# Moving stores from SyncE's queue to ScalarE's, pinning loads, and a diagonal-free spread in a streaming encoder layer

## The chip, the cores and the metric

The kernel runs on one core of a Trainium2 chip. Its time is the device time of one execution in microseconds (us); it is given as the median of several runs. A profile is one execution taken by the hardware profiler. The engines are PE (TensorE; PEld is its weight load), DVE (VectorE), ACT (ScalarE), POOL (GpSimd) and SP (SyncE, which here only issues DMAs). A DMA is issued by an instruction on an engine's own queue, SPq or ACTq; that instruction waits, in its place in the queue, until what it reads or overwrites is ready.

## The reference

One layer of a streaming encoder over 2048 prompt tokens and 64 sample tokens of width 1024, then a final RMSNorm. The first half mixes tokens (pooling and a matrix memory); the change leaves it as it is. The second half, which the change touches, is this:

```python
    h2 = rmsnorm(x, g2) * (1 + sc2) + sh2
    up = h2 @ w_up                      # 1024 -> 2 * 2816
    upp = jnp.concatenate([conv_buf.astype(up.dtype), up], 1)
    conv = b_conv + sum(w_conv[j] * upp[:, j:j + T] for j in range(CONV_W))
    a, g = jnp.split(conv, 2, -1)
    x = x + gt2 * ((jax.nn.silu(g) * a) @ w_down)
    ...
    y_prompt = rmsnorm(xp, g_final)
    y_sample = rmsnorm(xs, g_final)
```

`rmsnorm(x, g)` is x times the reciprocal root of its mean square over the 1024 features, times g. All is float32.

## The kernel before

Features lie on partitions and tokens run along the free dimension. The mixing half goes through four groups of 512 tokens and leaves the residual rows x in a DRAM tensor `x2d` (8 blocks of 128 features). The feed-forward half goes through three groups (`fgroups`, `o.g` = 0, 1, 2) of 704 tokens.

**Precision and pieces.** Every matmul operand is split into a high and a low part, and a product is three passes (`PASSES`) of float32r matmuls. A weight piece of 512 columns is loaded by SP, copied by ACT into its high part (`work_out`, L359), and DVE subtracts to get the low part (L362). The split piece lies in one of six buffers of the tag `wt`.

**The stream.** `stream` lists all weight pieces in the order in which PE wants them. `issue` starts the DMA of the next one: `w_up` and `w_down` pieces go through one of four `raw` buffers (L343), sums of `w_up` blocks (`wsum`) go straight into a `wt` buffer (L351), and pieces that were split before and kept come back whole (`wsplit`, L348). `pump` runs ahead: it splits the next few pieces and issues loads while fewer than six `wt` buffers are in use and at most seven pieces are pending. `get_unit` hands the next piece to PE, and `keep` (L367) stores it to DRAM if a later group is to load it whole. In group 0 of the feed-forward half two of the four `wsum` pieces of each feature block are kept this way, 44 stores of 512 KB.

**A pair.** For each of 22 feature blocks f, `Pair.products` computes the up projection of the a and g halves for 704 tokens with seven products in place of eight (sums of blocks, as in Strassen's scheme). A product is 12 matmuls of 352 columns (L1443). They follow each other as B11, B21, T4 of the pair before, T2, T3, B22, T1 (the first pair of a part has no T4). The kept pieces are those of T2 and T1. Between the products ACT copies PSUM banks (L1482, L1491, L1506), DVE adds and applies the convolution taps (L1451, L1495, L1431), ACT does scale and silu, and the result is split into `av`. `product` calls `pump` first, then `get_unit`, and after every second of its four blocks calls `tick(0)`.

**Parts.** The 22 blocks come in four parts (5, 5, 6, 6). After each part `down` multiplies its `av` by the `w_down` pieces (L1709), and `down_end` adds the result, times gt2, to the residual rows `x3` (L1724). `x3` has eight tiles, one buffer each (tags x0 to x7). `load_x2` (L1578) loads them from `x2d`: in group 0 two after each of the first pairs; in groups 1 and 2 two after each pair of part 0 once the list `bg[0]` is empty, and the rest at the end of part 0.

**Background work.** `bg` holds lists of generators; `tick(i)` runs the first one of list i up to its next `yield`, `drain` runs it to the end. `final`, for groups 0 and 1, is put into `bg[0]` at the end of a group and thus runs during part 0 of the next: it gets the mean square of each token (L1597), spreads the factor to all partitions, and for each of eight k multiplies `x3[k]` in place (DVE, L1606), stores it to the output `yT` (SP, L1608) and yields four times. `load_x2` for the next group therefore writes the very tile that L1608 reads. `prepare`, for groups 1 and 2, makes the next group's normed input and stores pieces of it from ACT (L784).

**The end.** The last part of group 2 does its down projection in two sections of tokens (`ENDS`, 448 and 256). `final_end` makes the output of a section; that of the first is ticked during the last five rows of the second, for every second of the six k of a row, and what is left runs in the last `drain`. It sums squares per token on PE (L1623), takes the factor `rs` on DVE and POOL (L1587, L1589), writes a diagonal matrix of it (DVE, L1630), multiplies it by ones on PE (L1637), which spreads the factor over the partitions, copies it (ACT, L1639), and multiplies the rows (DVE L1660, POOL L1656). `store` (L1652) sends them off.

**Order.** In the feed-forward half the instructions of PE, ACT, DVE and POOL stand in the order of the program (`tc.manual_schedule`, L1676), and so do the DMAs that ACT issues. The order of SP's queue is chosen by the framework's scheduler, which may move a DMA ahead of others that were traced before it. `tc.keep_in_program_order(ins)` ties an instruction behind the one traced before it on its engine.

Of the kernel before, what the change touches and what calls it, by code (L numbers as in the profile page):

```python
# [9 lines left out]
F32 = mybir.dt.float32  # L10
F32R = mybir.dt.float32r
AF = mybir.ActivationFunctionType
ALU = mybir.AluOpType
# [3 lines left out]
P = 128  # L17
D = 1024
KD = D // P
# [6 lines left out]
FT = 704  # L26
# [33 lines left out]
def tile_layer(ctx: ExitStack, tc: tile.TileContext, xT, vecs, cst, rst, rowv, w_mod, w_ada, w_qkou, w_v, w_pool,  # L60
               w_out, w_up, w_down, st_C, st_pool, yT, o_pool, o_C, o_m, o_conv):
    nc = tc.nc
    act, dve, pool, pe = nc.scalar, nc.vector, nc.gpsimd, nc.tensor
# [19 lines left out]
    def m2_ps():  # L83
        return bank("m2")
# [9 lines left out]
    def scr():  # L94
        return sp.tile([P, TMAX], F32, tag="scr", name="scr")
# [33 lines left out]
    ident = cp.tile([P, P], F32, tag="ident", name="ident")  # L129
# [9 lines left out]
    ones = ones_r.bitcast(F32)  # L139
# [91 lines left out]
    for g in range(NG):  # L231
        o = Grp()
# [70 lines left out]
    for g in range(NFG):  # L303
        for (f0, f1_) in PARTS:
# [8 lines left out]
            for i, (n, k) in enumerate(order):  # L313
                if i == f1_ - f0 - 2:
                    stream += late
                c = f0 + k // 4 * 4
# [9 lines left out]
    class Unit:  # L326

        state = 0
        w = raw = None
# [25 lines left out]
    def work_out(u, upto=2):  # L355
# [5 lines left out]
        if u.state == 1 and upto > 1:  # L361
            dve.tensor_tensor(out=u.w[:, 1, :u.n], in0=u.raw[:, :u.n], in1=u.w[:, 0, :u.n].bitcast(F32), op=ALU.subtract)  # L362
            u.state = 2

    def keep(u):
        if u.keep is not None:
            nc.sync.dma_start(out=u.keep, in_=u.w.bitcast(F32)[:, :, :u.n])  # L367

    def pump():

        while True:
            for i, u in enumerate(pend[:ahead[1]]):
                if u.w is not None or live[0] < ahead[2] or u.stays:
                    work_out(u, 2 if i < ahead[1] - ahead[3] else 1)
            if (pos[0] >= len(stream) or len(pend) >= ahead[0] or live[0] >= ahead[2]
                    or sum(u.w is None for u in pend) >= RB
                    or pos[0] < n_att and sum(u.w is not None for u in pend) >= WB - 2):
                break
            issue()
# [142 lines left out]
    x2d = dr.tile([KD, P, NTOK], F32, tag="x2d", name="x2d")  # L522
# [67 lines left out]
    for g in range(NFG):  # L590
        o = Grp()
# [8 lines left out]
    def fscr(dt=F32):  # L600
        if dt in ("rb", "ssum"):
            return spare[0].tile([P, FT], F32, tag=dt, name=dt)
        return spare[0].tile([P, FT], dt, tag="fscr", name="fscr", bufs=6)


    spare = []
# [182 lines left out]
    if True:  # L789
# [110 lines left out]
        h, pb = [], []  # L900
# [424 lines left out]
        for o in groups:  # L1325
# [14 lines left out]
            if o.g == 0:  # L1340
                dve.tensor_copy(M[:, GT + 1:GT + 2], RV[:, 2:3])
                dve.tensor_scalar(out=GH, in0=V[:, V_GH:V_GH + NH], scalar1=0.5, scalar2=None, op0=ALU.mult)
                t = scr()
                nc.sync.dma_start(out=t[:36, :512], in_=cst[:36, NCST + 512:NCST + 1024])
                dve.tensor_copy(E_r.rearrange("p h n -> p (h n)"), t[:36, :512])
                t = scr()
# [227 lines left out]
    def load_x2(o, ks=range(KD)):  # L1574
        x3 = []
        for k in ks:
            x = f2.tile([P, FT], F32, tag=f"x{k}", name=f"x{k}")
            nc.sync.dma_start(out=x, in_=x2d[k, :, o.t0:o.t0 + FT])  # L1578
            x3.append(x)
        return x3  # L1580

# [9 lines left out]
    def final(o, x3, ssum):  # L1591
        for _ in range(4):
            yield
        ps = m2_ps()
        tiles = [(t, min(P, FT - t)) for t in range(0, FT, P)]
        for ti, (t, n) in enumerate(tiles):
            pe.matmul(ps[:n, ti:ti + 1], ssum[:, t:t + n], ones[:, 0:1], start=True, stop=True)  # L1597
        stat_cols(ps, RF, [n for (t, n) in tiles])
        yield
        yield  # L1600
        box = []
        yield from bcast_cols(RF, 0, FT, box, fscr)
        yield
        yield
        for k in range(KD):
            dve.scalar_tensor_tensor(out=x3[k], in0=x3[k], scalar=V[:, V_GF + k:V_GF + k + 1], in1=box[0],  # L1606
                                     op0=ALU.mult, op1=ALU.mult)
            nc.sync.dma_start(out=yT[k, :, o.t0:o.t0 + FT], in_=x3[k])  # L1608
            for _ in range(4):
                yield  # L1610

    def final_end(o, x3, sums, lo, hi):

        w = hi - lo
        tiles = [(t, min(P, hi - t)) for t in range(lo, hi, P)]
        for _ in range(4 if lo == 0 else 0):
            yield
        ps = m2_ps()
        rs = f1.tile([P, 5], F32, tag="rs", name="rs", bufs=2)
        dg = fscr()  # L1620
        for ti, (t, n) in enumerate(tiles):
            for i, (sq, base) in enumerate(sums):
                pe.matmul(ps[:n, ti:ti + 1], sq[:, t - base:t - base + n], ones[:, 0:1], start=(i == 0),  # L1623
                          stop=(i == len(sums) - 1))
        stat_cols(ps, rs, [n for (t, n) in tiles])
        nf, rem = w // P, w % P
        blks = [(0, nf, P), (nf, nf + 1, rem)] if rem else [(0, nf, P)]
        for (a, b, n) in blks:
            v = dg[:n, a * P:a * P + (b - a) * n].rearrange("p (t c) -> p t c", c=n)
            dve.tensor_tensor(out=v, in0=ident[:n, :n].unsqueeze(1).broadcast_to([n, b - a, n]),  # L1630
                              in1=rs[:n, a:b].unsqueeze(2).broadcast_to([n, b - a, n]), op=ALU.mult)
        for _ in range(4 if lo == 0 else 0):
            yield
        pb = m2_ps()
        for (a, b, n) in blks:
            c = slice(a * P, a * P + (b - a) * n)
            pe.matmul(pb[:, c], ones[:n, :], dg[:n, c], start=True, stop=True)  # L1637
        rb = fscr()
        act.activation(rb[:, :w], pb[:, :w], AF.Copy)  # L1639
        YG = ((0, 1), (1, 3), (3, 5), (5, 6), (6, 8))  # L1640
        y = {}
        for (a, b) in YG:
            if a % 2 == 0 or b - a == 2:
                t = f1.tile([P, XT], F32R, tag="hx", name="y", bufs=2 * len(BN)).bitcast(F32)[:, :3 * w].rearrange(
                    "p (k t) -> p k t", t=w)
                j = 0
            for k in range(a, b):
                y[k] = (t, j)
                j += 1

        def store(a, b):
            (nc.sync if a < 5 else nc.scalar).dma_start(  # L1652
                out=yT[a:b, :, o.t0 + lo:o.t0 + hi].rearrange("k p t -> p k t"), in_=y[a][0][:, y[a][1]:y[a][1] + b - a, :w])
        if lo > 0:
            for k in (5, 6, 7):
                pool.tensor_tensor(out=y[k][0][:, y[k][1], :w], in0=x3[k][:, lo:hi], in1=rb[:, :w], op=ALU.mult)  # L1656
        for (a, b) in YG:
            for k in range(a, b):
                if k < 5 or lo == 0:
                    dve.tensor_tensor(out=y[k][0][:, y[k][1], :w], in0=x3[k][:, lo:hi], in1=pb[:, :w], op=ALU.mult)  # L1660
                    if lo == 0:
                        yield
                        yield
            store(a, b)
        yield
# [11 lines left out]
    x3, ssum = [], None  # L1677
    for o in fgroups:
        Bo = B[o.g]
        for pi, (f0, f1_) in enumerate(PARTS):  # L1680
            nf = f1_ - f0
# [4 lines left out]
            for f in range(f0, f1_):  # L1686
                old, pair = pair, Pair(o, Bo, f, f - f0, av)
                pair.products(old)
                if o.g == 0 and len(x3) < KD or pi == 0 and not bg[0]:
                    x3 += load_x2(o, range(len(x3), min(len(x3) + 2, KD)))  # L1690
            if pi == 0 and o.g > 0:
                drain(0)
                x3 += load_x2(o, range(len(x3), KD))
# [76 lines left out]
        if not o.last:  # L1770
            drain(1)
            bg[0].append(final(o, x3, ssum))
            x3 = []
# [84 lines left out]
```

## Time and profile before

| what | value |
|---|---|
| median of 3 runs | 2237.66 us (2231.12 to 2242.47) |
| the profiled execution | 2240.48 us, span 2238.7 us |
| granted TensorE clock, mean | 0.994 |
| DMA | 493.52 MB, mean 220 GB/s |
| kept pieces stored from SP in group 0 (`wsplit<-wt`) | 44 of 512 KB |
| output rows stored from SP in groups 1 and 2 (`yT<-x`) | 16 of 352 KB |
| residual rows loaded (`x<-x2d`) | 24 of 352 KB |

The span runs from the first to the last instruction; the execution's own time is a little longer. A row of the busy times gives us, share of the span and count. A row of the waits says which line on which engine stood idle, what ended the wait, how long in all, how often, and the longest. A row of the timeline begins with start and duration; the square bracket holds the idle time before it. For DMAs the time from issue to landing is counted apart from the issuing instruction.

### The profile page before, as it was taken

How to read it: one execution, taken by the hardware profiler on the slowest of the kernel's cores; microseconds unless marked ns; L12 is line 12 of the kernel's file. 1: busy time of each engine (PE TensorE's matmuls, PEld its weight loads, DVE VectorE, ACT ScalarE, POOL GpSimd, SP SyncE). 2: the span in 40 equal slices, each digit the busy share in tenths (PEclk: the TensorE clock that was granted, in tenths of full speed). 3: DMA queues.
4: the chain of work that ended last, by engine and by line, in shares of the span. 5: the costliest groups of instructions: out<-in, count | busy, mean ns of one | idle time of the engine just before them, and what ended most of it. 6: DMA issues, size and time to landing. Idle time of an engine off the chain costs nothing.

```text
span 2238.7 us, 38008 instructions
## 1 busy us (share of the span) xinstructions
PE 2196.5 (98%) x13720; PEld 2082.8 (93%) x13720; DVE 1577.7 (70%) x2860; ACT 1002.1 (45%) x1992; POOL 284.2 (13%) x524
## 2 busy tenths in 40 slices
PE   8999999999999999999999999999999999999998
PEld 6778888878898999999999999999999999999997
DVE  4868668667755688687868677687757685757474
ACT  3544335234234356464636445445435353435254
POOL 0122012111200130010100110000001210101012
PEclk9999999999999999999999999999999999999999
DMA  9967986997888477556746964556458554353442
GB/s 351 328 231 244 342 296 230 316 305 249 272 293 273 155 241 250 191 194 240 227 157 214 300 226 165 201 187 224 142 171 267 192 201 160 114 174 123 144 151 79
DMA packets 276444, 493.52 MB, mean 220 GB/s; under 512 B 24952, under 2 KB 103416, under 8 KB 276256
## 3 DMA queue, kind: packets, MB, share of 16 engines
q1 hardware_dynamic: 266784, 468.77, 62.4%
q10 hardware_dynamic: 9472, 22.32, 2.6%
q8 instruction: 108, 1.77, 0.3%
q14 instruction: 80, 0.66, 0.1%
HBM read 382.77 MB, written 108.22 MB: 219 GB/s over the span
## 4 chain that ended last, share of the span: by engine, by line
PE 83%; DMA 8%; DVE 5%; issue 2%; ACT 1%; SPq 1%; POOL 0%; POOLq 0%; DVEq 0%; ACTq 0%
PE mm L1443 38%; PE mm L1709 22%; PE mm L415 17%; DMA raw<-w_ada 2%; PE mm L1038 1%; DMA wsum<-w 1%; DMA wt<-wsum 1%; DMA wt<-hl_kept 1%; DMA hl_kept<-wt 1%; DVE acc L196 1%; DMA w<-w_ada 1%; PE m L1222 1%; PE mm L969 1%; PE m L1221 1%; PE m L1302 1%
## 5 line engine op out<-in xcount | busy, mean ns | idle before, releaser
L1443 PE MATMUL mm<-hx,wt 128*128 128x352 f32 x5544 | 886.2, 321 | 5.8 <-ACT wt L359 3.7
L1443 PEld LDWEIGHTS mm<-hx,wt 128*128 128x128 f32 x5544 | 880.7, 188 | 7.0 <-ACT wt L359 4.3
L1709 PE MATMUL mm<-av,wt 128*128 128x352 f32 (+2 forms) x3168 | 508.1, 321 | 0.0
L1709 PEld LDWEIGHTS mm<-av,wt 128*128 128x128 f32 x3168 | 502.7, 188 | 1.8 <-DVE x L1724 0.3
L415 PE MATMUL mm<-hl,wt 128*128 128x512 f32 (+2 forms) x1920 | 399.8, 361 | 4.9 <-DMA wt<-hl_kept 3.8
L362 DVE TENSOR_TENSOR wt<-raw,wt 128x512 fp32r<-128x512 f32 (+3 forms) x494 | 309.3, 642 | 90.6 <-ACT wt L359 85.5
L415 PEld LDWEIGHTS mm<-hl,wt 128*128 128x128 f32 x1920 | 316.6, 190 | 54.7 <-issue 8.5
L359 ACT ACTIVATE wt<-raw 128x512 fp32r<-128x512 f32 (+3 forms) x494 | 271.1, 570 | 189.0 <-PE mm L1709 81.0
L1724 DVE SCALAR_TENSOR_TENSOR x<-mm,MOD,x 128x352 f32<-128x352 f32 (+4 forms) x224 | 106.4, 525 | 114.8 <-PE mm L1709 114.8
L415 PE MATMUL mm<-mx,wt 128*128 128x512 f32 (+2 forms) x960 | 185.7, 353 | 1.5 <-DVE wt L362 1.3
L415 PEld LDWEIGHTS mm<-mx,wt 128*128 128x128 f32 x960 | 158.7, 188 | 26.6 <-DVE wt L362 1.5
L1431 DVE SCALAR_TENSOR_TENSOR tg<-eg,V,tg 128x704 f32<-128x704 f32 (+1 forms) x132 | 125.6, 952 | 45.6 <-ACT tg L1426 43.2
L362 DVE TENSOR_TENSOR wt<-wt 128x512 fp32r<-128x512 f32 x176 | 122.6, 697 | 45.5 <-ACT wt L359 45.5
L359 ACT ACTIVATE wt<-wt 128x512 fp32r<-128x512 f32 x176 | 110.1, 626 | 74.0 <-DMA wt<-wsum 65.7
L1431 DVE SCALAR_TENSOR_TENSOR ta<-ea,V,ta 128x704 f32<-128x704 f32 (+1 forms) x132 | 125.6, 952 | 8.5 <-ACT ta L1426 6.2
L1566 DVE TENSOR_TENSOR av<-tg,av 128x704 fp32r<-128x704 f32 (+4 forms) x112 | 62.1, 588 | 47.7 <-ACT av L1558 47.5
L196 DVE SCALAR_TENSOR_TENSOR acc<-raw,CA,acc 128x512 f32<-128x512 f32 x84 | 62.4, 775 | 41.2 <-DMA raw<-w_ada 41.2
L1537 ACT ACTIVATE tg<-tg 128x704 f32<-128x704 f32 (+1 forms) x66 | 52.4, 794 | 79.1 <-DVE tg L1431 79.1
L1451 DVE TENSOR_TENSOR eg<-mm,u 128x352 f32<-128x352 f32 x154 | 70.1, 467 | 22.8 <-ACT u L1506 11.2
L1491 ACT ACTIVATE u<-mm 128x352 f32<-128x352 f32 x66 | 30.5, 462 | 120.2 <-PE mm L1443 82.5
L1038 PE MATMUL mm<-wt,hl 128*128 128x256 f32 (+1 forms) x576 | 71.4, 282 | 2.5 <-DVE scr L578 2.5
L1038 PEld LDWEIGHTS mm<-wt,hl 128*128 128x128 f32 x576 | 69.3, 188 | 3.6 <-DVE scr L578 2.7
(281 smaller groups left out, 2030.5 us busy)
## 6 DMA issues: line engine op xcount, KB each, us to landing
wt<-hl_kept SPq DMA_DIRECT2D x108, 512.0 KB, 6.0
raw<-w_up SPq DMA_DIRECT2D x198, 256.0 KB, 3.1
wt<-wsum SPq DMA_DIRECT2D x176, 256.0 KB, 4.1
wt<-wsplit SPq DMA_DIRECT2D x88, 512.0 KB, 4.0
raw<-w_down SPq DMA_DIRECT2D x96, 256.0 KB, 2.9
w<-w_up SPq DMA_DIRECT2D x88, 256.0 KB, 4.1
wsum<-w SPq DMA_DIRECT2D x44, 512.0 KB, 4.3
wsplit<-wt SPq DMA_DIRECT2D x44, 512.0 KB, 4.8
```

Of the source, the lines that this page charges most:

```text
L196: dve.scalar_tensor_tensor(out=acc[s], in0=w, scalar=CA[:, k, s:s + 1], in1=acc[s], op0=ALU.mult, op1=ALU.add)
L359: act.activation(u.w[:, 0, :u.n], u.raw[:, :u.n], AF.Copy)
L362: dve.tensor_tensor(out=u.w[:, 1, :u.n], in0=u.raw[:, :u.n], in1=u.w[:, 0, :u.n].bitcast(F32), op=ALU.subtract)
L415: pe.matmul(ps[bi][:, :hi - lo], U[:, a, k % 4 * P:(k % 4 + 1) * P], mv[k][:, b, lo:hi], start=(at == 0 and pi == 0), stop=(k == order[-1] ...
L1038: pe.matmul(ps[ti][:n, :cols], h[4 * kh + k4][:, b, lo:lo + n], U[:, a, k4 % 2 * cols:(k4 % 2 + 1) * cols], start=(kh == 0 and k4 == 0 and ...
L1431: dve.scalar_tensor_tensor(out=t[:, :E], in0=ext[:, j:j + E], scalar=wc(j, f), in1=t[:, :E], op0=ALU.mult, op1=ALU.add)
L1443: pe.matmul(ps[:, :FH], U[:, a, kc * P:(kc + 1) * P], Bo.at(nm, kc, b), start=(first and kc == 0 and pi == 0), stop=(kc == 3 and pi == 2), ...
L1451: dve.tensor_tensor(out=ext[:, d:d + b - a], in0=ps[:, a:b], in1=u[:, a:b], op=ALU.add)
L1537: act.activation(self.tg[:, :E], self.tg[:, :E], AF.Silu)
L1566: dve.tensor_tensor(out=cut(1), in0=self.of_tg(cut(0), a, b), in1=cut(0).bitcast(F32), op=ALU.subtract)
L1709: pe.matmul(ps[i][:, :hi - lo], U[:, a, k % 4 * P:(k % 4 + 1) * P], av[k](b, lo, hi), start=(k == 0 and (a, b) == PASSES[0]), stop=(k == n ...
L1724: dve.scalar_tensor_tensor(out=x3[n][:, a:b], in0=ps[i][:, a - lo:b - lo], scalar=gt2(n, s), in1=x3[n][:, a:b], op0=ALU.mult, op1=ALU.add)
```

## The change

There are four edits, all of the feed-forward half.

1. `keep` no longer stores at once in this half. It puts the piece on the list `owed`, and the next `pump`, that is, the beginning of the next product, issues the store from ACT (`settle`). In the mixing half (`spare` still empty) nothing changes.
2. In `load_x2` the loads of groups 1 and 2 are tied behind what SP was given before them, and three rows in place of two follow each pair.
3. In `final` the store of an output row is issued by ACT, one yield after its product; the yields stay four in all.
4. In `final_end` the diagonal matrix is left out: one matmul per 128 tokens takes the column of factors, repeated 128 times, as the stationary operand and the identity as the moving one. For the first section one of four yields ahead of the spread goes, and one of two after each row.

```diff
+    owed = []
+
     def keep(u):
-        if u.keep is not None:
+        if u.keep is None:
+            return
+        if spare:
+            owed.append(u)
+        else:
             nc.sync.dma_start(out=u.keep, in_=u.w.bitcast(F32)[:, :, :u.n])
 
+    def settle():
+        while owed:
+            u = owed.pop(0)
+            act.dma_start(out=u.keep, in_=u.w.bitcast(F32)[:, :, :u.n])
+
     def pump():
 
+        settle()
         while True:
...
             x = f2.tile([P, FT], F32, tag=f"x{k}", name=f"x{k}")
-            nc.sync.dma_start(out=x, in_=x2d[k, :, o.t0:o.t0 + FT])
+            got = nc.sync.dma_start(out=x, in_=x2d[k, :, o.t0:o.t0 + FT])
+            if o.g > 0:
+                tc.keep_in_program_order(got)
...
-            nc.sync.dma_start(out=yT[k, :, o.t0:o.t0 + FT], in_=x3[k])
-            for _ in range(4):
+            yield
+            act.dma_start(out=yT[k, :, o.t0:o.t0 + FT], in_=x3[k])
+            for _ in range(3):
                 yield
...
-        dg = fscr()
...
-        nf, rem = w // P, w % P
-        blks = [(0, nf, P), (nf, nf + 1, rem)] if rem else [(0, nf, P)]
-        for (a, b, n) in blks:
-            v = dg[:n, a * P:a * P + (b - a) * n].rearrange("p (t c) -> p t c", c=n)
-            dve.tensor_tensor(out=v, in0=ident[:n, :n].unsqueeze(1).broadcast_to([n, b - a, n]),
-                              in1=rs[:n, a:b].unsqueeze(2).broadcast_to([n, b - a, n]), op=ALU.mult)
-        for _ in range(4 if lo == 0 else 0):
+        for _ in range(3 if lo == 0 else 0):
             yield
         pb = m2_ps()
-        for (a, b, n) in blks:
-            c = slice(a * P, a * P + (b - a) * n)
-            pe.matmul(pb[:, c], ones[:n, :], dg[:n, c], start=True, stop=True)
+        for ti, (t, n) in enumerate(tiles):
+            pe.matmul(pb[:, t - lo:t - lo + n], rs[:n, ti:ti + 1].broadcast_to([n, P]), ident[:n, :n],
+                      start=True, stop=True)
...
                     if lo == 0:
                         yield
-                        yield
...
-                    x3 += load_x2(o, range(len(x3), min(len(x3) + 2, KD)))
+                    x3 += load_x2(o, range(len(x3), min(len(x3) + (3 if o.g else 2), KD)))
```

## The prediction

> **What bounds the kernel now.** First the page's busy times, then busy time by stretch (columns: stretch, length, then busy time and count of PE, PEld, DVE, ACT, POOL, then granted clock, share of the DMA engines, GB/s), then PE's own waits.
>
> ```profile
> PE 2196.5 (98%) x13720; PEld 2082.8 (93%) x13720; DVE 1577.7 (70%) x2860; ACT 1002.1 (45%) x1992; POOL 284.2 (13%) x524
> ...
> 828.70:1291.00 462.30, 461.45 (x2912) 461.00 (x2913) 351.39 (x565) 242.12 (x423) 46.16 (x97) 1.00 0.66 221
> 1291.00:1758.50 467.50, 465.19 (x2926) 464.60 (x2925) 333.48 (x538) 218.91 (x390) 38.14 (x97) 1.00 0.59 198
> 1758.50:2226.90 468.40, 466.98 (x2946) 464.70 (x2944) 313.26 (x591) 208.96 (x392) 62.38 (x191) 1.00 0.43 145
> 2217.00:2239.00 22.00, 12.43 (x89) 10.79 (x89) 9.76 (x27) 4.87 (x11) 6.87 (x10) 0.77 0.38 131
> ```
>
> The feed-forward half is the three stretches from 828.7, one per group of 704 tokens. PE is busy in all but 0.85, 2.31 and 1.42 us of them: TensorE bounds this half, and the change takes no work worth counting off TensorE. So it can win only those idle microseconds, what follows from them, and part of the tail, where PE is busy 12.43 of 22. PE's waits in narrow windows name the idle time (waiting line, what it waited for, us, times, longest):
>
> ```profile
> PE mm L1443 <- DVE ea L1495: 0.8, 1, 0.8
> PE mm L1443 <- ACT wt L359: 2.3, 1, 2.3
> PE mm L1443 <- ACT wt L359: 1.4, 1, 1.4
> ```
>
> These are the window 938 to 950 (group 0), 1285 to 1340 (group 1) and 1755 to 1830 (group 2). The second is followed by a slow stretch:
>
> ```profile
> 1331.30:1334.70 3.40, 3.40 (x14) 3.40 (x13) 3.40 (x5) 1.42 (x2) 0.49 (x1) 0.50 0.95 298
> 1797.20:1800.60 3.40, 3.40 (x22) 3.40 (x23) 3.37 (x5) 1.67 (x3) 1.35 (x2) 1.00 0.96 339
> ```
>
> After the 2.3 us stall the granted clock is 0.50 for 3.4 us: 14 matmuls where an equal stretch (second row, behind the stall of group 2) holds 22. The 1.4 us stall is followed by clock 1.00, the second row. Now why PE waits at 1330, from the timeline (start, us, engine; SPq is SyncE issuing DMAs) and SP's waits from 1291 to 1331 (first waits row) and 1759 to 1798 (second):
>
> ```profile
> 1312.05 0.32 SPq L1578 DMA_DIRECT2D x<-x2d  x1
> 1312.46 0.39 SPq L1608 DMA_DIRECT2D yT<-x  x1
> ...
> 1316.35 0.32 SPq L1578 DMA_DIRECT2D x<-x2d  x1
> ...
> 1317.50 0.95 DVE L1606 SCALAR_TENSOR_TENSOR x<-x,V,rb 128x704 f32<-128x704 f32 x1
> 1317.73 0.37 SPq L351 DMA_DIRECT2D wt<-wsum  x1
> ...
> 1318.73 0.47 ACT L1506 ACTIVATE u<-mm 128x352 f32<-128x352 f32 x1 [1.01 <-PE mm L1443]
> ...
> 1324.49 0.63 ACT L359 ACTIVATE wt<-wt 128x512 fp32r<-128x512 f32 x1 [2.71 <-DMA wt<-wsum]
> ...
> SPq L1578 <- DMA yT<-x: 8.9, 3, 4.3
> ...
> SPq L1578 <- DMA yT<-x: 11.2, 4, 3.7
> ```
>
> SP issues everything in one order. A residual row's load (L1578) goes into the buffer from which the group before stores its output (L1608), so SP stands until that store has landed: 8.9 us in three waits. Behind it stands the load of a weight piece (L351), issued at 1317.73; ACT starts on it at 1324.49, everything ACT does then is late, and PE stalls. Group 2 repeats it.
>
> **The change, part by part.**
>
> *Output stores on ACT, residual loads pinned late.* The 16 stores of L1608 leave SP, and the loads of L1578 in groups 1 and 2 stand where they are traced: three after the fourth pair, three after the fifth, two right behind. By then the stores have landed, so both kinds of SP wait go. I take the stall of group 1 at 2.3, plus its slow clock at 1.5 (8 of 22 matmuls missing is 1.2 us of 3.4; half clock for 3.4 us would be 1.7): 3.8 us. Group 2: 1.4 us.
>
> The Trainium skill, "TensorE: Matmul & The Clock Gate", section "HAM oscillation", puts its rule as no PE idle gaps over about 3.4 us. By it a 2.3 us gap would not slow the clock and the sum would be 1.5 less; the trace has 0.50 behind this gap, and the trace decides.
>
> What the added waits hold up: a store on ACT waits for its DVE product, and behind it stand ACT's copies of PSUM and its weight pieces. It is traced one yield (six matmuls) behind the product. The tightest row above: DVE ends L1606 at 1318.45, ACT's next copy starts at 1318.73 on PE's word. Issue takes 0.34 to 0.43 us, as now on SP:
>
> ```profile
> L1608 SPq DMA_DIRECT2D yT<-x x16: 338/382/427, 1306.2 to 1803.2; - x16
> ...
> L1724 DVE SCALAR_TENSOR_TENSOR x<-mm,MOD,x x16: 570/576/584, 1378.2 to 1403.8; 128x352 f32<-128x352 f32 x16
> ...
> DMA to landing us min/median/max: 2.0/5.2/8.7
> ```
>
> So a copy may slip by some 0.5 us; ACT is busy 219 of 467 us in group 1 and PE comes back to that bank two products later, so I cost it at nothing (if the cover is gone: 0.5 for each of 16, 8 us). The pinned loads are first used at 1378.2 (second row, the first group-1 use of L1724). Counted in products of 1.90 us (below), the fourth pair ends near 1345 and the fifth near 1358, so even 8.7 us to landing (third row, the DMAs of this tensor) leaves 10 us or more. Cost nothing; if five loads in a row hold the w_down loads behind them, the stall comes back here, at most once a group.
>
> *Kept weight pieces stored by ACT (group 0).* 44 stores leave SP:
>
> ```profile
> SPq L367 <- DVE wt L362: 113.7, 30, 6.6
> SPq L351 <- PE mm L1443: 30.0, 38, 3.4
> ...
> L367 SPq DMA_DIRECT2D wsplit<-wt x44: 319/320/535, 830.9 to 1239.6; - x44
> ...
> DMA to landing us min/median/max: 2.8/4.9/8.1
> ...
> 897.38 1.90 PE mm L1443 x12
> ...
> 1040.93 22.18 PE mm L1443 x140
> ...
> 1055.31 6.96 SPq L367 DMA_DIRECT2D wsplit<-wt  x2
> ...
> 1061.10 0.45 ACT L1491 ACTIVATE u<-mm 128x352 f32<-128x352 f32 x1
> 1061.45 0.96 ACT L1426 ACTIVATE tg<-eg,V 128x704 f32<-128x704 f32 x1
> ```
>
> Gone is 113.7 us of SP standing for DVE. But PE lost only 0.8 us in this group, so between 0 and 0.8 can come of it; I take 0.4, the middle, since the weight load behind that stall had a 512 KB store issued ahead of it. ACT gets 44 x 0.32 = 14 us of issuing in a group where it is idle 220 of 462: nothing.
>
> The hidden cost is the weight buffer. There are six; loads already wait for PE to free one (30.0 us). One product is 12 matmuls and 1.90 us. In the pairs from 1040.93 the tenth product is of the second kind of kept piece, so PE leaves that buffer at 1059.9. SP stored the piece as soon as DVE had split it, at 1055.31, and at 4.9 us to landing the store was done by 1060.2. ACT stores it at the start of the product after, behind the two ACT rows, so at about 1062.4, and the buffer is free at 1067.3, some 7 us later than PE leaves it. Two of seven pieces a pair go this way, so for most of a pair five buffers do the work of six. Followed through the order of the code, the piece that takes the late buffer is needed five products (9.5 us) after PE left it; store, landing, ACT's copy and DVE's split take 2.5 + 4.9 + 0.6 + 0.7 = 8.7. It fits with 0.8 us to spare here, where ACT runs 1.2 late behind PE, and with 2 where it doesn't. Cost nothing at the median; the bound is a rival.
>
> *The tail.* The last sections' scale factor is spread over partitions without the diagonal matrix, and the first section's rows come at half the yields:
>
> ```profile
> 2227.66 2.20 DVE L1660 TENSOR_TENSOR y<-x,m 128x448 f32<-128x448 f32 x4
> ...
> 2228.71 0.36 PE L1623 MATMUL m<-ones_r,fscr 128*128 128x1 f32 x2
> ...
> 2229.78 0.15 DVE L1587 TENSOR_SCALAR rs<-m 128x2 f32<-128x2 f32 x1
> 2230.01 0.71 POOL L1589 TENSOR_TENSOR rs<-rs,half 128x2 f32<-128x2 f32 x1 [3.03 <-DVE rs L1587]
> 2230.75 0.42 DVE L1630 TENSOR_TENSOR fscr<-ident,rs 128x256 f32<-128x256 f32 x1 [0.82 <-POOL rs L1589]
> ...
> 2231.32 1.19 PE L1637 MATMUL m<-fscr,ones_r 128*128 128x256 f32 x2 [2.25 <-DVE fscr L1630]
> ```
>
> Without L1630 the matmuls start at 2230.75 and not at 2231.32: 0.57. Four rows of the first section (2.20 us of DVE) lie ahead of L1587: it starts at 2229.78, 0.71 after PE's statistic ends at 2229.07. With 15 ticks in the last five rows and 15 yields instead of 24 these four are done earlier: 0.7 won, of which I give back 0.2, as three rows and not two now fall within the last row's matmuls, ahead of DVE's own work there. The matmuls become four of 128 columns for two of 256: equal columns, two more weight loads, 0.1 (bounds 0 and 0.6, half of the 1.19 of now). Tail: 0.6 + 0.7 - 0.2 - 0.1 = 1.0 us (0.4 to 1.3).
>
> **Sum.** 3.8 + 1.4 + 0.4 + 1.0 = 6.6 us. The profiled execution took 2240.48 us for a span of 2238.7, so this one would take 2233.9; the median of the runs shown is 2.8 lower at 2237.66, which gives 2231.1.
>
> **Rivals.**
>
> *Only half of the stalls goes.* Against the forecast: the load of 1317.73 took 6.7 us to land, and the engines are at 0.95 load near there, so a load issued earlier may still be late; the stores stay in that stretch, only on another queue. For it: the residual loads leave, and two waits (4.3 the longest) go. Half of 5.2 and the tail: 3.6 us, 2234.1.
>
> *The late buffer stalls group 0.* Place: ACT's first step on the piece that takes a buffer under store. It decides where a store lands over 5.7 us after issue (4.9 + 0.8); the median of now is 4.9, the longest 8.1. Price: 2.4 for a pair at 8.1, so 53 for all 22 pairs of the group, 13 for one in four. With that, 13 - 6.6 is 6.4 us slower than before, 2244.1. Against it: ACT follows PE more closely once SP no longer stands before the loads, and a store that is alone on its queue may land sooner.
>
> *Loads slowed by ACT's stores.* A store on its own queue no longer takes its turn behind SP's loads but runs beside them. If each pair lost what group 0's one stall cost, 22 x 0.8 = 17.6 us, the time is 11.0 over before, 2248.7. Against it: from 960 to 1285 the kernel already stores from ACT beside these loads, and PE is busy all of it:
>
> ```profile
> 960.00:1285.00 325.00, 325.00 (x2052) 324.83 (x2051) 250.81 (x400) 171.40 (x299) 31.95 (x67) 1.00 0.67 222
> L784 ACTq DMA_DIRECT2D Bd<-fscr x56: 326/327/791, 922.9 to 1619.0; - x56
> ```
>
> This is the Trainium skill's rule, "DMA: Bandwidth & Descriptors", section "Queues, rings and completion order": each DMA engine takes turns between queues, packet by packet.
>
> **Chances.** Forecast (gain of 4.5 to 9) 0.52; half of the stalls (0 to 4.5) 0.22; late buffer 0.17; slowed loads 0.04; more than 9, if SP's freedom shows elsewhere too, 0.05. The runs of before lie from 2231.12 to 2242.47, so a median moves by some 3 us by itself. 2225 to 2245 leaves out the worse halves of the two slow cases and the gains over 12, 0.2 at most. About 0.5% (11 us) is what a measurement of this kernel tells from no change: faster by more takes the last case or a lucky median, 0.09; slower by more the worse half of both slow cases, 0.10; the rest 0.81.
>
> **What would show it.** Right: no SP wait of L1578 for yT; no PE wait and clock 1.00 near 1330 and 1796; L1587 right behind L1623 at the end, the last matmuls right behind POOL. Wrong: in group 0 ACT or SP waits for wsplit stores, with PE waits at L1443 in many pairs; new PE waits at L1709 from 1346 to 1380; ACT copies late behind its own stores.

## The result and the profile after

The median went from 2237.20 us (11 runs, 2231.12 to 2242.47) to 2250.14 us (11 runs, 2239.03 to 2258.20). The ratio is 1.0054, 95% interval 1.0043 to 1.0066, so the change costs 10 to 15 us. The profiled execution took 2250.78 us for a span of 2249.0. The line numbers have moved: the up matmul L1443 is now L1455, the down matmul L1709 is L1716, the store of kept pieces L367 is L378 on ACT, the output store L1608 is L1623 on ACT, the residual load L1578 is L1590.

Windows of equal work show where the time went. The first fence is after, the second before (stretch, length, then busy time and count of PE, PEld, DVE, ACT, POOL, granted clock, DMA share, GB/s). In each, the rows are group 0; part 0 of group 1, up and then down projection; part 0 of group 2, up and then down.

```profile
826.43:1302.45 476.02, 467.03 (x2920) 462.61 (x2919) 353.07 (x569) 241.94 (x423) 48.55 (x97) 1.00 0.64 215
...
1302.45:1375.28 72.83, 71.99 (x456) 71.41 (x455) 56.92 (x85) 36.60 (x64) 8.77 (x23) 1.00 0.64 213
1375.28:1412.49 37.21, 36.66 (x228) 35.77 (x227) 28.00 (x55) 14.95 (x32) 0.37 (x2) 1.00 0.56 184
1769.51:1842.52 73.01, 71.96 (x456) 71.41 (x455) 58.26 (x103) 37.04 (x70) 16.42 (x43) 1.00 0.65 212
1842.52:1878.31 35.79, 35.73 (x224) 35.19 (x223) 20.28 (x46) 9.68 (x21) 0.61 (x4) 1.00 0.40 131
```

```profile
827.04:1291.74 464.70, 462.68 (x2920) 461.93 (x2919) 353.05 (x569) 242.12 (x423) 46.16 (x97) 1.00 0.66 221
...
1291.74:1367.36 75.62, 73.31 (x456) 73.02 (x455) 57.03 (x85) 36.94 (x64) 8.78 (x23) 0.98 0.63 217
1367.36:1403.23 35.87, 35.87 (x228) 35.87 (x227) 27.98 (x55) 15.04 (x32) 0.93 (x2) 1.00 0.52 170
1759.23:1832.37 73.14, 71.72 (x457) 71.43 (x455) 58.08 (x103) 37.25 (x70) 16.45 (x43) 1.00 0.65 224
1832.37:1867.54 35.17, 35.17 (x224) 35.17 (x223) 20.17 (x46) 9.86 (x21) 1.18 (x4) 1.00 0.34 108
```

Group 0 is longer by 476.02 - 464.70 = 11.3 us, and so accounts for the whole loss of the profiled execution (2250.78 - 2240.48 = 10.3). Its matmuls are as many, its weight loads (PEld) take as long and the clock is 1.00: TensorE does the same work at the same speed and stands in between. The weight loads leave 476.02 - 462.61 = 13.4 us idle where they left 464.70 - 461.93 = 2.8. PE's own busy time is 4.4 us longer with as many matmuls, so part of the standing is counted there as busy. In group 1 the slow clock of before (0.98 in that row) is gone and the up projection is 2.8 shorter, but the down projection behind it is 1.3 longer. Group 2 wins 0.1 and loses 0.6.

What SP and PE waited for in group 0, after (three rows each), and then the SP row of before that belongs beside the third (line, releaser, us in all, times, longest):

```profile
SPq L343 <- DVE wt L362: 197.0, 108, 9.1
SPq L351 <- PE mm L1455: 66.1, 40, 4.0
SPq L351 <- DMA wsplit<-wt: 38.0, 16, 4.1
...
PE mm L1455 <- DVE ea L1507: 4.6, 6, 1.5
PE mm L1455 <- DVE wt L362: 2.4, 4, 1.2
PE mm L1455 <- ACT u L1503: 1.6, 1, 1.6
```

```profile
SPq L351 <- DMA wsplit<-wt: 3.4, 4, 1.8
```

SP's 113.7 us of standing for DVE before a store are gone. SP now stands elsewhere: 38.0 us, where it was 3.4, with a weight load (L351) in its hand whose buffer is still being read by a store of a kept piece. PE waits eleven times where it waited twice; the two of before (1.2 and 0.8 us) are among the eleven, and the nine new ones are 6.7 us together. The chain of waits shows one such stall from end to end (start, us, what):

```profile
1057.26 0.02 ACT u L1518
...
1057.33 6.75 DMA wsplit<-wt
...
1064.13 3.17 DMA wt<-wsum
...
1067.33 0.02 ACT wt L359
...
1067.86 0.45 ACT u L1503
...
1072.48 5.48 DMA wsplit<-wt
1077.98 4.58 DMA wt<-wsum
```

ACT issues the store at 1057.33, behind its PSUM copy (L1518). The store lands 6.75 us later. Only then can SP issue the load into that buffer, and this takes 3.17 us to land. ACT splits the piece at 1067.33, 10.0 us after the store began; its copy of PSUM (L1503) comes behind that, and PE, which waits for the copy, stands 1.6 us, the third PE row above. Then the same pair of transfers follows again: 5.48 and 4.58. Followed back in the same way, the nine new waits lead to three such stores, those of 840.92, 949.42 and 1057.33: four of them (1.5, 0.6, 1.6 and 0.6 us) stand right behind a store and the load after it, five (2.4 us in all) further down the same chains, behind loads that had become late.

### The profile page after: what moved, and what is told of

It reads as the page before. It is cut to its first block, busy times and chain, and to the rows that moved or that the text cites. A ratio compares the mean times of both kernels' runs of the same rounds, so it can differ in the third digit from the quotient of the medians.

```text
span 2249.0 us, 37961 instructions
## 1 busy us (share of the span) xinstructions
PE 2202.3 (98%) x13726; PEld 2082.0 (93%) x13726; DVE 1579.9 (70%) x2857; ACT 1002.5 (45%) x1992; POOL 282.7 (13%) x524
## 3 DMA queue, kind: packets, MB, share of 16 engines
q8 instruction: 108, 1.77, 0.3%
## 4 chain that ended last, share of the span: by engine, by line
PE 78%; DMA 10%; DVE 6%; ACT 2%; issue 2%; SPq 1%; POOL 0%; ACTq 0%; POOLq 0%; DVEq 0%
PE mm L1455 33%; PE mm L1716 20%; PE mm L427 18%; DMA wt<-wsum 2%; DMA raw<-w_ada 1%; PE mm L1050 1%; DMA wsplit<-wt 1%; DMA wsum<-w 1%; DVE wt L362 1%; PE mm L981 1%; DMA Bd<-fscr 1%; DMA wt<-hl_kept 1%; DVE acc L196 1%; PE m L1211 1%; PE m L1234 1%
## 5 line engine op out<-in xcount | busy, mean ns | idle before, releaser
L1455 PE MATMUL mm<-hx,wt 128*128 128x352 f32 x5544 | 889.6, 321 | 11.6 <-DVE ea L1507 5.5
L1455 PEld LDWEIGHTS mm<-hx,wt 128*128 128x128 f32 x5544 | 879.4, 188 | 17.5 <-ACT u L1503 6.1
L1716 PE MATMUL mm<-av,wt 128*128 128x352 f32 (+2 forms) x3168 | 509.7, 321 | 0.6 <-DVE av L1578 0.3
L1716 PEld LDWEIGHTS mm<-av,wt 128*128 128x128 f32 x3168 | 502.8, 188 | 3.8 <-DVE av L1578 0.9
L1731 DVE SCALAR_TENSOR_TENSOR x<-mm,MOD,x 128x352 f32<-128x352 f32 (+4 forms) x224 | 106.5, 527 | 112.3 <-PE mm L1716 112.2
L1443 DVE SCALAR_TENSOR_TENSOR tg<-eg,V,tg 128x704 f32<-128x704 f32 (+1 forms) x132 | 125.7, 952 | 50.2 <-ACT tg L1438 47.9
L1443 DVE SCALAR_TENSOR_TENSOR ta<-ea,V,ta 128x704 f32<-128x704 f32 (+1 forms) x132 | 125.7, 952 | 8.8 <-ACT ta L1438 6.0
L1578 DVE TENSOR_TENSOR av<-tg,av 128x704 fp32r<-128x704 f32 (+4 forms) x112 | 62.1, 589 | 43.5 <-ACT av L1570 43.3
L1503 ACT ACTIVATE u<-mm 128x352 f32<-128x352 f32 x66 | 30.4, 461 | 116.3 <-PE mm L1455 76.1
```

What stands on the lines that cost most here:

```text
L1443: dve.scalar_tensor_tensor(out=t[:, :E], in0=ext[:, j:j + E], scalar=wc(j, f), in1=t[:, :E], op0=ALU.mult, op1=ALU.add)
L1455: pe.matmul(ps[:, :FH], U[:, a, kc * P:(kc + 1) * P], Bo.at(nm, kc, b), start=(first and kc == 0 and pi == 0), stop=(kc == 3 and pi == 2), ...
L1578: dve.tensor_tensor(out=cut(1), in0=self.of_tg(cut(0), a, b), in1=cut(0).bitcast(F32), op=ALU.subtract)
L1716: pe.matmul(ps[i][:, :hi - lo], U[:, a, k % 4 * P:(k % 4 + 1) * P], av[k](b, lo, hi), start=(k == 0 and (a, b) == PASSES[0]), stop=(k == n ...
L1731: dve.scalar_tensor_tensor(out=x3[n][:, a:b], in0=ps[i][:, a - lo:b - lo], scalar=gt2(n, s), in1=x3[n][:, a:b], op0=ALU.mult, op1=ALU.add)
```

## The experiments

No kernel leaves out any of the computation. Each ratio is to runs of the kernel before on the same chip, side by side. The columns of the table are lengths in us of windows like those above: group 0, part 0 of groups 1 and 2, and from the start of the last down projection to the end.

| kernel | group 0 | g1 up | g1 down | g2 up | g2 down | end | ratio (95%) |
|---|---|---|---|---|---|---|---|
| before | 464.70 | 75.62 | 35.87 | 73.14 | 35.17 | 57.27 | 1 |
| after | 476.02 | 72.83 | 37.21 | 73.01 | 35.79 | 56.82 | 1.0054 (1.0043 to 1.0066) |
| e1: after, edit 1 undone | 466.14 | 72.81 | 37.26 | 73.02 | 36.06 | 56.29 | 1.0010 (1.0001 to 1.0018) |
| e2: after, ACT stores early | 468.79 | 72.81 | 37.58 | 73.00 | 36.39 | 56.80 | 1.0017 (1.0008 to 1.0027) |
| e3: edit 1 alone | 478.01 | 72.59 | 35.87 | 75.11 | 35.20 | 57.27 | 1.0061 (1.0044 to 1.0077) |
| e4: edit 2 alone | 466.49 | 71.47 | 37.32 | 71.48 | 35.95 | 56.74 | 0.9994 (0.9984 to 1.0005) |
| e5: edit 2 spread over three pairs | 466.59 | 72.06 | 35.89 | 72.97 | 35.17 | 57.29 | 0.9989 (0.9979 to 0.9999) |
| e6: e1, output stores later | 464.90 | 71.48 | 38.00 | 71.47 | 36.11 | 56.83 | 0.9994 (0.9985 to 1.0003) |
| e7: edit 4 alone | 466.17 | 73.39 | 35.87 | 72.99 | 35.18 | 56.79 | 0.9992 (0.9980 to 1.0004) |
| e8: e5 with edit 4 | 466.47 | 72.01 | 35.90 | 72.75 | 35.17 | 56.30 | 0.9985 (0.9975 to 0.9995) |
| e9: e6, last two rows loaded later | 464.87 | 71.48 | 35.87 | 71.48 | 35.17 | 56.29 | 0.9978 (0.9967 to 0.9990) |
| e10: e9 with output stores on SP | 464.95 | 71.48 | 35.87 | 71.47 | 35.18 | 56.79 | 0.9977 (0.9968 to 0.9986) |

Group 0 is the same program in e1 and in e4 to e10 as before, and its length scatters from 464.7 to 466.6: differences under 2 us there say nothing, and the loss of after in this group is 9 to 11 us.

**e1, kept pieces back on SP.** The theory from the trace was the held weight buffer; the rivals, ACT's time for issuing and contention between two queues.

```diff
-        if spare:
-            owed.append(u)
-        else:
-            nc.sync.dma_start(out=u.keep, in_=u.w.bitcast(F32)[:, :, :u.n])
+        nc.sync.dma_start(out=u.keep, in_=u.w.bitcast(F32)[:, :, :u.n])
```

> The changed kernel with one edit undone: the kept weight pieces of group 0 are stored by SP again, where the scheduler puts them; output stores on ACT, pinned loads and the tail stay changed. Group 0 took 464.5 us before and 476.0 after (start of its up projection to that of group 1). Every theory that blames the stores on ACT expects group 0 back at 464 to 465 and the whole kernel 11 us faster than the changed one, ratio to before 0.998 to 1.000. If the 11 us came from elsewhere (pinned loads, output stores, tail), group 0 stays near 476.

Group 0 is back at 466.14, within the scatter of before, and the ratio at 1.0010, just above the expected range. The loss belongs to edit 1; edits 2 to 4 together gain nothing.

**e2, the same stores on ACT, but earlier.** ACT issues the store at the start of the product after the piece's split, two products (3.8 us) sooner than in after. The queue, the number and the size of the stores stay.

```diff
             u.state = 2
+            if spare and u.keep is not None:
+                owed.append(u)
+                u.owes = True
...
-        if u.keep is None:
+        if u.keep is None or u.owes:
             return
```

> The changed kernel, but ACT stores a kept piece one product after DVE has split it, two products (3.8 us) earlier than in the changed kernel; still 44 stores of 512 KB on ACT's own queue. Theory of the held buffer (a weight load waits until the store of the piece before it in the buffer has landed): SP's waits for wsplit stores fall from 38.0 us to under 10, and group 0 comes back from 476.0 to 464 to 468. Rival, ACT's order and queue (44 issues in ACT's instruction stream, or stores that run beside the loads): the waits for landings may go, but group 0 stays at 472 or more.

SP's wait for these stores in group 0 (the load is L353 in this kernel):

```profile
SPq L353 <- DMA wsplit<-wt: 4.3, 6, 1.3
```

38.0 us have become 4.3, and 7.2 of the 11.3 us are gone, with every store still on ACT's queue. Group 0 is 0.8 over the range of the theory and 3 under that of the rival. So most of the loss comes from the time at which the buffer is free again, not from the queue. Group 0 stays 2.2 above the longest with SP's stores (466.6), and what makes that is open. The chains of the three longer waits that are left in e2, at 860, 950 and 1070, hold no store of a kept piece. In each of them ACT starts on a weight load 6.4 to 7.8 us after its issue. A rival that no run separates is the order of SP's queue. When the stores left SP, the framework's scheduler placed SP's 266 other DMAs of group 0 anew: written down by tensor, in order, after differs from before in 74 of the 266 places, e2 in 55, and after and e2 differ from each other in 57.

**e3, edit 1 alone in the kernel before.**

> The kernel before with only the first edit: kept pieces stored by ACT at the next pump. Theory that this edit alone makes the loss: group 0 at 474 to 478 against 464.5, groups 1 and 2 and the tail as before, ratio 1.004 to 1.006. Rival, that the loss needs the other edits too: group 0 under 470.

478.01 us in group 0 and a ratio of 1.0061, at the upper end of what was expected: edit 1 makes the loss without the others. Groups 1 and 2, which this edit doesn't touch, are not as before, though: their up projections take 72.59 and 75.11 us where the profile of before has 75.62 and 73.14. The stall and the slow clock behind it are there again, but this time in group 2 (PE waits 1.8 us, and the clock is 0.50 from 1810.40 to 1813.80).

**e4, edit 2 alone**, output stores still on SP.

> The kernel before with only the pinned loads (three after a pair in groups 1 and 2); output stores stay on SP. Part 0 of group 1 took 75.62 us of up projection before and 72.83 after, that of group 2 73.14 and 73.01. Theory that the SP wait for the landing of an output store was the whole stall: group 1 at 71.6 to 72.3 and group 2 at 71.6 to 72.0, that is better than the changed kernel, whose ACT stores hold ACT up; the down projection behind group 1 a little longer, as in the changed kernel (37.2 against 35.9). Ratio 0.997 to 0.999. Rival, that the stores of DVE's rows on SP block as well: part 0 of group 1 stays over 74.

The up projections are at 71.5 us in both groups: the whole stall goes with the residual loads, though SP still issues the output stores and stands for DVE in front of them. But the down projection behind is 1.4 and 0.8 longer, and the ratio, 0.9994, can't be told from 1, where 0.997 to 0.999 was expected. SP's queue in this kernel, from its timeline, and what ACT waited for during that down projection of group 1 (first waits row; the second is e5's):

```profile
1352.09 10.19 SPq L343 DMA_DIRECT2D raw<-w_down  x4
1362.34 2.33 SPq L1578 DMA_DIRECT2D x<-x2d  x5
1364.77 14.60 SPq L343 DMA_DIRECT2D raw<-w_down  x6
```

```profile
ACT wt L359 <- DMA raw<-w_down: 6.1, 4, 2.8
```

```profile
ACT wt L359 <- DMA raw<-w_down: 3.0, 2, 1.7
```

Three loads behind the fifth pair and the two "right behind" stand in a row, 1.8 MB ahead of the next six loads of w_down pieces. ACT waits 6.1 us for those pieces where it waits 3.0 without the burst; the av splits behind it are late, and PE stands.

**e5, the same loads spread over three pairs** (three, three, two).

```diff
-                if o.g == 0 and len(x3) < KD or pi == 0 and not bg[0]:
+                if o.g == 0 and len(x3) < KD or pi == 0 and o.g > 0 and f >= 2:
```

> The kernel before with edit 2 alone, but the pinned residual loads of groups 1 and 2 go out three behind the third pair, three behind the fourth and two behind the fifth, so that no five stand in a row. Theory (the five loads in a row hold the w_down loads behind them on SP's queue): the down projection behind part 0 of group 1 goes from 37.3 us with edit 2 alone back to 35.9, that of group 2 from 36.0 to 35.2, the up projections of part 0 stay at 71.5, and the time is some 2.2 us lower than with edit 2 alone, a ratio of 0.998 to before. Rival (eight residual loads ahead of the w_down loads cost this wherever they stand, by their bytes): 37.3 and 36.0 stay, ratio 0.9994.

The burst theory holds: 35.89 and 35.17, as before. Part of the gain is lost again in front of that, 0.6 and 1.5 us in the up projections, which were expected to stay at 71.5: three residual loads are now issued at the third pair, among the last output stores and ahead of a weight load. The timeline of SP and ACT in group 1:

```profile
1334.89 1.98 SPq L1578 DMA_DIRECT2D x<-x2d  x3
1336.97 0.38 SPq L351 DMA_DIRECT2D wt<-wsum  x1
...
1343.22 0.63 ACT L359 ACTIVATE wt<-wt 128x512 fp32r<-128x512 f32 x1 [3.33 <-DMA wt<-wsum]
```

The weight load has landed when ACT starts on it, 6.2 us after its issue, and ACT has stood 3.33 us for it. As in before, where the same took 6.7 us, ACT is late behind a weight load. But SP's waits in this stretch name no landing of an output store: here the stall comes without one, with three residual loads sent right ahead of the weight load.

**e6, output stores on ACT three yields behind their product** and not one; kept pieces on SP.

```diff
-            yield
-            act.dma_start(out=yT[k, :, o.t0:o.t0 + FT], in_=x3[k])
             for _ in range(3):
                 yield
+            act.dma_start(out=yT[k, :, o.t0:o.t0 + FT], in_=x3[k])
+            yield
```

> Edits 2, 3 and 4 (kept pieces stored by SP), but ACT's output store stands three yields behind its product on DVE and not one. Theory (ACT stands for DVE's product in front of the store, and its PSUM copies are late): the up projection of part 0 goes from 72.8 to 71.5 us in group 1 and from 73.0 to 71.5 in group 2, no PE gap of 0.9 or 1.2 us there, ratio 0.9998 to before where the kernel with one yield has 1.0010. Rival (the 0.34 us that ACT needs to issue each of the 16 stores): the store still takes its 0.34, and 72.8 and 73.0 stay.

72.81 and 73.02 become 71.48 and 71.47. In after, ACT stands in front of its own store until DVE's product (L1620) is done, and what is queued behind is late. First two of ACT's waits in part 0 of group 1 of after, which e6 doesn't have, then the chain of after, then ACT's timeline in e6 at the same place:

```profile
ACT tg L1549 <- DVE x L1620: 2.8, 1, 2.8
...
ACT s L1494 <- DVE x L1620: 1.9, 1, 1.9
```

```profile
1342.17 0.87 DVE x L1620
...
1343.07 0.34 ACTq L1623
...
1345.69 0.96 DVE x L1620
...
1346.67 0.34 ACTq L1623
...
1347.05 0.47 ACT s L1494
```

```profile
1333.15 0.46 ACT L1491 ACTIVATE s<-mm 128x352 f32<-128x352 f32 x1 [1.44 <-PE mm L1452]
1333.26 0.34 ACTq L1621 DMA_DIRECT2D yT<-x  x1
```

In after the copy of PSUM (L1494) starts at 1347.05, right behind the store, which DVE released at 1346.65. In e6 the same copy (L1491) is released by PE, and the store goes out without a wait. It takes the same 0.34 us: the issue costs PE nothing here, the wait in front of it did. Of the 1.3 us won in group 1, 0.7 are lost again in the down projection behind it, 38.00 against 37.26; why it is longer than in e1, with the same five loads in a row, is open.

**e7, edit 4 alone.**

> The kernel before with edit 4 alone. Forecast of the prediction: the end comes 1.0 us sooner. By the trace of after: 1.2 won between PE's last statistic and the last spread, 0.6 given back in front of that statistic (PE waits for POOL's and ACT's squares, which follow DVE's first-section rows), so 0.6. The last down projection with what follows is then 56.7 us (56.3 by the forecast) beside 57.3 before, both at a half clock at the very end; the ratio, 0.9996 to 0.9998, can hardly be told from 1. Rival: the rows of the first section delay the last row's own work by as much as is won: 57.3.

The end is 56.79 us against 57.27, 0.5 won; the ratio can't be told from 1. The table has two lengths of the end for each version, by the clock: without edit 4 57.27 to 57.29 at a mean clock of 0.92 (before, e3, e5) and 56.74 at 0.94 (e4), with it 56.79 to 56.83 at 0.93 (after, e2, e6, e7, e10) and 56.29 to 56.30 at 0.95 (e1, e8, e9). Long compared with long and short with short, edit 4 gains 0.4 to 0.5. The groups are those of before, and they show the stall of group 1 a second time: PE waits 1.7 us at the same line, and the stretch behind it runs at full clock (before had 2.3 and 0.50).

```profile
PE mm L1443 <- ACT wt L359: 1.7, 1, 1.7
```

```profile
1329.90:1333.30 3.40, 3.40 (x23) 3.40 (x22) 3.40 (x6) 1.78 (x3) 0.49 (x1) 1.00 0.99 293
```

**e8, e5 and e7 together.**

> The kernel before with edit 4 and with edit 2 spread over three pairs; all stores stay on SP. If the parts add up: 4.1 us from group 1's stall and its slow clock, 1.7 from group 2's, 0.6 from the end, nothing lost, so 6.4 us faster than before, a ratio of 0.997. If the cost behind part 0 of groups 1 and 2 (1.4 and 0.8 us) stays in spite of the spreading: 4.2 us, 0.998.

0.9985, near the second case's 0.998 but not for its reason: the cost behind part 0 is gone (35.90 and 35.17), and the up projections keep the stalls of e5 (72.01 and 72.75), which neither case had.

**e9 and e10, the last two residual rows loaded inside the down projection**, behind its third row; e9 is e6 with this, e10 has edits 2 and 4 with the output stores on SP.

```diff
                 drain(0)
-                x3 += load_x2(o, range(len(x3), KD))
...
             do(9)
+            if pi == 0 and o.g > 0:
+                x3 += load_x2(o, range(len(x3), KD))
             for n in range(NE):
```

> Edits 2, 3 and 4 with kept pieces stored by SP and ACT's output store three yields behind its product, as in the run before this one; beside that the last two residual rows are loaded inside the down projection, behind its third row, and not right behind three others. If the costs found so far are separate: up projection of part 0 71.5 us in groups 1 and 2, down projection behind it 35.9 and 35.2, last down projection 56.3 to 56.8; groups 1 and 2 together 942.3 where before's profile has 946.9, ratio 0.9978 to before. Rival (the w_down loads are held by three loads in a row as well, or the two rows come too late inside the down projection): 37 to 38 us stays behind part 0, ratio 0.9994 as without the move.

> The same with the output stores on SP, as before: edits 2 and 4 and the last two residual rows loaded inside the down projection. The stores keep SP standing for DVE (12.9 us in groups 1 and 2 each) but the residual loads come behind all of them, so the same times are expected as with late stores on ACT: 71.5, 35.9 and 35.2, groups 1 and 2 together 942.3, ratio 0.9978. Rival (moving the stores off SP is what frees the weight loads): slower than the run with ACT's late stores by more than 1.5 us.

Both came out as the separate costs had it: no loss left in part 0 of either group, ratios of 0.9978 and 0.9977. They beat the kernel before by 2.2 to 7.4 and 3.1 to 7.2 us. The rival that moving output stores off SP is what frees the weight loads falls: e10 keeps them there.

## Why the prediction was wrong

**Kept pieces on ACT, the step that failed.** "It fits with 0.8 us to spare here" rests on "store, landing, ACT's copy and DVE's split take 2.5 + 4.9 + 0.6 + 0.7 = 8.7". Between the landing of the store and ACT's copy there is another transfer, the load that fills the buffer again, and its own landing was left out. The chain of waits has both in a row, 6.75 and 3.17, then 5.48 and 4.58. The times to landing in group 0, first of these stores after, then of the loads after, then of the loads before:

```profile
L378 ACTq DMA_DIRECT2D wsplit<-wt x44: 326/326/360, 833.9 to 1255.3; - x44
...
DMA to landing us min/median/max: 2.6/3.5/6.9
```

```profile
L351 SPq DMA_DIRECT2D wt<-wsum x87: 319/327/1692, 826.6 to 1300.7; - x87
...
DMA to landing us min/median/max: 2.9/4.0/6.5
```

```profile
L351 SPq DMA_DIRECT2D wt<-wsum x87: 319/333/2082, 827.2 to 1290.0; - x87
...
DMA to landing us min/median/max: 3.0/4.5/7.3
```

With the medians of after (the trace has the landing of 30 of the 44 stores and of 54 of the 87 loads) and 0.3 for the issue, an estimate is 2.5 + 3.5 + 0.3 + 4.0 + 0.6 + 0.7 = 11.6 us against the 9.5 that were there: 2.1 late, not 0.8 early. With the 4.5 of before it could have been seen beforehand: 8.7 + 0.3 + 4.5 = 13.5. Taken two products (3.8 us) earlier, as in e2, the 11.6 become 7.8, or 9.6 with e2's own medians of 4.7 for the stores and 4.6 for the loads: level with the 9.5, and most of the loss went, not all of it.

**The rival that came nearest** was the late buffer, at 0.17. Its price of 13 us for one pair in four is close to the 11.3 measured, but by luck: it was made of 2.4 us in each such pair, and the new waits are nine of 0.3 to 1.6 us. Its place was wrong by one step: it is SP that stands, in front of the load, and not ACT's first step. The prediction's own sign of being wrong names the right place, SP's waits for wsplit stores with PE waits at the up matmul, and this is what came. The rival's condition, a store that lands over 5.7 us after its issue, was too kind by the same missing term: the median store landed in 3.5 and the loss came all the same. *Loads slowed by ACT's stores* falls for after: the loads landed in 4.0 us where they took 4.5 before. For what is left in e2, where they took 4.6, it is not ruled out.

**The 0.4 of group 0** never showed. SP was freed of 113.7 us of standing for DVE, and even with the stores early (e2) group 0 is not shorter than before. The Trainium skill, "DMA: Bandwidth & Descriptors", section "Issuing engines are not separate DMA queues", says that starting DMAs from several engines saves only the time on the sequencer. For the output stores these runs agree: e10 with SP (0.9977) and e9 with ACT (0.9978) are level.

**Stalls of groups 1 and 2.** That pinning the residual loads ends them was right. How much of a stall was SP's standing for a landing and how much the residual loads' company right ahead of a weight load is not separated: e5, without that standing, still loses 0.6 and 1.5. Against the profile of before e4 shows 75.62 - 71.47 = 4.1 (predicted 3.8) and 73.14 - 71.48 = 1.7 (predicted 1.4). But 1.5 of the 3.8 was the slow clock, which e7 doesn't have behind a wait of 1.7 us: its up projection is 73.39, and against that the gain is 1.9. In e3 it is group 2 that has the slow clock. For both groups together e4 is 5.8 us shorter than before, 4.7 than e3 and 3.4 than e7, so the predicted 5.2 lies within what single executions show. The slow clock was read off one execution and belongs to some of them. The clock fell to 0.50 behind PE waits of 2.3 us (before) and of 2.2 and 1.77 us (e3, groups 0 and 2), and stayed at 1.00 behind 1.85 (e2, group 0) and 1.7 (e7). So the length of the wait alone doesn't decide, and what does was not measured. The Trainium skill's rule quoted in the prediction ("TensorE: Matmul & The Clock Gate", section "HAM oscillation") speaks of gaps over about 3.4 us. The waits of this case that were followed by a slow clock are all shorter, and the measurement decides.

**"So a copy may slip by some 0.5 us ... I cost it at nothing"** was wrong, if by little: with the store one yield behind its product the copies slip, and the up projections lose 72.81 - 71.48 = 1.3 us in group 1 and 1.5 in group 2 (e1 against e6). The slack was read at one row, where DVE's product ended 0.28 us before ACT's next copy. At two other stores of group 1 ACT came there before DVE's product was done and stood 2.8 and 1.9 us for it; PE's waits in the up projections of after reach 0.6 us in group 1 and 0.9 in group 2.

**"If five loads in a row hold the w_down loads behind them, the stall comes back here"** did happen, for 1.4 and 0.8 us, and was a condition that the forecast had left at nothing.

**The tail** was forecast at 1.0 and gave 0.5. Its timeline in after, and two rows of before that belong beside the first and the third:

```profile
2232.60 5.29 PE L1716 MATMUL mm<-av,wt 128*128 128x256 f32 x42
...
2236.98 1.68 DVE L1668 TENSOR_TENSOR y<-x,m 128x448 f32<-128x448 f32 x3
...
2238.57 0.61 DVE L1731 SCALAR_TENSOR_TENSOR x<-mm,MOD,x 128x192 f32<-128x192 f32 x2
...
2240.21 0.36 PE L1637 MATMUL m<-ones_r,fscr 128*128 128x1 f32 x2
2240.61 0.16 DVE L1601 TENSOR_SCALAR rs<-m 128x2 f32<-128x2 f32 x1 [1.43 <-PE m L1637]
2240.85 0.71 POOL L1603 TENSOR_TENSOR rs<-rs,half 128x2 f32<-128x2 f32 x1 [2.40 <-DVE rs L1601]
2241.61 1.22 PE L1644 MATMUL m<-ident,rs 128*128 128x128 f32 x4 [1.04 <-POOL rs L1603]
```

```profile
2222.53 4.57 PE L1709 MATMUL mm<-av,wt 128*128 128x256 f32 x36
...
2227.13 0.61 DVE L1724 SCALAR_TENSOR_TENSOR x<-mm,MOD,x 128x192 f32<-128x192 f32 x2 [0.49 <-PE mm L1709]
```

From the end of PE's statistic to the spread it is 2241.61 - 2240.57 = 1.04 us where before had 2231.32 - 2229.07 = 2.25: 1.2 won, where the forecast had 0.6 + 0.7. The four matmuls take 1.22 against 1.19, 0.03 of the 0.1 put down for them. The give-back was mis-sized: three rows of the first section (from 2236.98) hold up DVE's own work for the last row. DVE starts on that work (L1731) at 2238.57, 0.68 after PE's last down matmul ends at 2237.89; in before it started 0.03 after it (2227.10, 2227.13). So 0.7 is given back and not 0.2, and of the 1.2 only 0.5 is left.

The sum: 3.4 to 5.8 us of stalls and 0.5 at the end are what edits 2 and 4 can give, and e9 and e10 gained 0.0022 x 2241 = 4.9 us. The change as it stands spends this on late copies and the burst (e1 is at 1.0010), and with edit 1 it loses 9 to 11 us more in group 0, most of it by the held buffer.

## What to carry to other kernels

When a store is moved to a later place, follow the buffer that it reads until it is full again: two landings stand in series there, that of the store and that of the load behind it, and every step of that way must be in the sum. A DMA that waits for compute should be issued late enough that it needn't wait, on whichever queue it is; on a compute engine the wait holds up that engine's own work. And loads moved out of one jam make another where they land in a row: give them gaps as well.

## What the runs showed of the hardware

The kept pieces landed about as soon from ACT's queue as from SP's: a median of 3.5 us in after and 4.7 in e2, where the prediction's row has 4.9 and e1, with SP, 4.3. The weight loads beside them had 4.0 and 4.6, against 4.5 in before. An issue of a DMA that need not wait took ACT 0.33 to 0.34 us, with no effect that these runs could tell (e9 against e10). The granted clock halved for 3.4 us behind PE waits of 2.3 us (before) and of 2.2 and 1.77 us (e3), and stayed at 1.00 behind waits of 1.85 (e2) and 1.7 (e7).
